# A hybrid GLA/HGRN2 diffusion layer: the work around the ends of the up-projection, and the out-projection's operand loads, in another order

## The chip, the cores and the metric

The kernel runs on one core of a Trainium2 chip. The metric is the device time of one execution in microseconds (us). The engines are TensorE (PE; its weight loads are listed apart as PEld), VectorE (DVE), ScalarE (ACT), GpSimd (POOL) and SyncE (SP, which here only issues DMAs).

## The reference

One layer of a diffusion backbone: 1024 sample tokens (a latent grid of width 64) and 128 prompt tokens, model width 1024, FFN width 2816.

```
def trunk_layer(x, mod, s_gla, s_hgrn, ...):
    shift1, scale1, gate1, shift2, scale2, gate2 = jnp.split(mod, 6, axis=-1)
    h = rmsnorm(x, norm1) * (1 + scale1) + shift1
    mix, new_gla, new_hgrn = hybrid_mixer(h, s_gla, s_hgrn, ...)
    x = x + gate1 * mix
    h = rmsnorm(x, norm2) * (1 + scale2) + shift2
    x = x + gate2 * conv_ffn(h, w_ffn_up, ffn_conv, b_ffn_conv, w_ffn_down, grid)

def hybrid_mixer(...):     # 4 GLA heads and 4 HGRN2 heads, both directions
    q_a, k_a, v_a, g_a, lr_a, q_b, f_b, i_b, g_b = jnp.split(h @ w_in, offsets, axis=-1)
    o_a, ... = bidir_scan(...);  o_h, ... = bidir_scan(...)
    merged = jnp.concatenate([o_a * silu(g_a), o_h * silu(g_b)], axis=-1)   # each normed first
    return merged @ w_out, new_gla, new_hgrn

def conv_ffn(h, w_up, conv_w, conv_b, w_down, grid):
    u = dw_conv(h @ w_up, conv_w, conv_b, grid)     # 3x3 over the grid, width 3 for the prompt
    gate, up = jnp.split(u, 2, axis=-1)
    return (jax.nn.silu(gate) * up) @ w_down
```

The layer's result goes through a last rmsnorm. mod is a product of the conditioning vector (one for the samples, one for the prompt) with w_ada.

## The kernel before

**Precision.** Every large product is made from three fp32r matmuls: both operands are split into a high part, rounded to fp32r, and the rest, and high·high, high·low and low·high are added in PSUM. A *split* is thus one ScalarE copy (L132 or L1736 for weights) and one subtraction, `split_lo` (L69), on VectorE or POOL. Names ending in h and l are the two parts.

**Stages, in the order of time:**
1. Modulation, first norm, first projections (to some 135 us).
2. The scan: six groups of heads in `ORDER` over three token blocks. Between its small matmuls (L944 lv, L1005 and L1012 for the states) the generator `stream` feeds large ones as filling: projections (L612, L626), and in the last group the out-projection (`fill_steps`, L692, matmuls L755). Weights come by a list `seq` in whose order SP loads them (`load_w`, L115), each split as soon as it is issued. `issue_after` binds an instruction behind another one; the rest of the order is left to a scheduler and to the pools.
3. The second norm and the first operands of the up stage (some 700 to 772 us).
4. The up stage: 22 columns of 128 hidden units (c = 0 to 21). A column's product is done by seven half-size products in the Strassen-Winograd manner, `up(c, p)` with p = 1 to 7, 12 matmuls each (L1751), over combined weights (slots "11", "12", "21", "22" and the sums s1 to s4) and combined token blocks (t1 to t4). `up_prompt` (L1979) does the prompt in two halves, and `prompt_columns` transposes its result. F and S are the two PSUM tiles of a column (gate and up halves); to finish them VectorE adds copies p1, u2 and p5, which ScalarE makes (L1943), L2070 and L2071 for F and L2090 for S (in column 0 `first_sums`, L1825). Product 4 of a column runs in the next column's time. Then the convolution (`conv_rows`, L1899: one ScalarE product and eight VectorE steps L1915 for each tile, `conv_prompt` L1925), silu, and POOL's product of the two halves (L2011), which goes to scratch in DRAM (scr_g). POOL also forms the sums of two columns' tokens (L1868 to L1871, scr_s) and splits the next column's weights. For column 0 the sequence on each engine is fixed by `run(engine, fn)`, which chains each instruction behind the engine's last.
5. The down stage: again seven products, of 11 pairs of columns with 12 matmuls each (`product`, L2197, matmuls L2208), whose operands are loaded in pairs and split; then the prompt (L2259), gates, the last norm.

**The places the change touches.** In group 5 of the scan (n == 5), the last w_in column (3616 + 3P) is loaded and split like the others. `fill_steps` waits for three reloaded w_out tiles `ws`, then for pairs of merged scan outputs `ms` (tag mh) and four more w_out tiles, and builds the gate of the first residual by two matmuls of a one-hot row with the modulation (L737), copied by ScalarE (L738). It then goes through six token tiles, halves, and seven f of three matmuls. For the down stage, `load_gates` (L2127) brings the modulation rows to SBUF and `make_gates` (L2131) builds four half gates by matmuls (L2139) and copies (L2140), in the middle of the first product (beside its pair 10).

The core of the loop around the scan's filling and of a split:

```
for part in range(2):
    with tc.issue_after(last.ins):
        if part == 0:
            states.step("keys")
...
nc.scalar.activation(hi, raw, AF.Copy)
split_lo(eng, lo, raw, hi)
```

## Time and profile before

| | us |
|---|---|
| median of three runs | 1539.32 (1538.26 to 1544.63) |
| the profiled execution | 1542.7 |
| its span | 1540.9 |
| PE busy in it | 1483.3 |
| DVE, ACT, POOL busy | 1147.4, 783.7, 710.4 |
| steady up stage, 860 to 1257 | PE 397.00 of 397.00 |

How to read the rows that follow in the prediction: a row of the timeline gives the start and the duration in us, the engine, the line, the operation, its output and input, the shape, and how many instructions were put together; in brackets stands how long the engine had been idle before it and which instruction, or DMA, ended that idle time. A row of the waits gives the total, how often, and the longest. A row of the windows gives for a stretch its length, the busy time of PE, PEld, DVE, ACT and POOL with the number of instructions, then the TensorE clock that was granted (1.00 is full), the mean busy share of the 16 DMA engines, and GB/s. SPq is SP issuing a DMA.

### The profile page before, as it was taken

What the parts mean: (1) busy time and instruction counts of PE and PEld (TensorE: products, weight loads), DVE (VectorE), ACT (ScalarE), POOL (GpSimd) and SP (SyncE); (2) the same over time, 40 slices, a digit from 0 to 9 for tenths busy, and PEclk for the clock granted to TensorE, in tenths of its full rate; (3) what the DMA queues carried; (4) which work ended last, traced back from release to release, by engine and by line L of the source; (5) the groups of instructions that cost most, each with busy time, mean ns of one, the idle gap of its engine ahead of it and who ended that gap; (6) DMA issues with size and microseconds to landing.
All of it is one profiled execution on the core that took longest, in us unless ns stands there. A gap on an engine that the chain in (4) does not pass through costs nothing.

```text
span 1540.9 us, 31129 instructions
## 1 busy us (share of the span) xinstructions
PE 1483.3 (96%) x12506; PEld 1258.1 (82%) x12506; DVE 1147.4 (74%) x1731; ACT 783.7 (51%) x1523; POOL 710.4 (46%) x538
## 2 busy tenths in 40 slices
PE   7999999999999999899989999999999999999997
PEld 2899989999898988677767888888888887788886
DVE  3666566665566667655689999999999999479575
ACT  3565666455454545513664444444444444467444
POOL 1512132334232240122238999999999987000001
PEclk9999999999999999999999999999999999999999
DMA  9312112336445352777641655554654665979762
GB/s 339 129 41 58 36 53 79 98 108 207 114 135 170 120 184 87 274 282 252 219 151 58 218 148 125 134 130 123 193 137 119 198 169 175 333 243 365 243 192 116
DMA packets 172939, 252.49 MB, mean 164 GB/s; under 512 B 11732, under 2 KB 113602, under 8 KB 170874
## 3 DMA queue, kind: packets, MB, share of 16 engines
q1 hardware_dynamic: 149591, 172.21, 35.0%
q0 software_dynamic: 22592, 77.60, 16.3%
q8 instruction: 98, 1.61, 0.4%
q10 hardware_dynamic: 611, 0.68, 0.1%
q14 instruction: 47, 0.39, 0.1%
HBM read 190.62 MB, written 82.90 MB: 178 GB/s over the span
## 4 chain that ended last, share of the span: by engine, by line
PE 80%; DMA 6%; DVE 5%; ACT 3%; issue 3%; POOL 2%; SPq 1%; ACTq 0%; POOLq 0%; DVEq 0%
PE u L1751 26%; PE mm L612 15%; PE xb L2208 6%; PE yb L2208 6%; PE mm L626 5%; PE x L1979 4%; PE mm L755 3%; PE lv L944 3%; PE yb L2259 2%; PE u L1521 2%; PE x L1012 2%; DVE acc L1915 2%; DMA raw<-in_w_in_dram 1%; PE mm L506 1%; DMA mh<-scr_m 1%
## 5 line engine op out<-in xcount | busy, mean ns | idle before, releaser
L1915 DVE SCALAR_TENSOR_TENSOR acc<-u,convc,acc 128x945 f32<-128x945 f32 (+2 forms) x352 | 426.8, 1218 | 7.8 <-ACT acc L1903 0.7
L69 POOL TENSOR_TENSOR wl<-raw,wh 128x1024 fp32r<-128x1024 f32 x42 | 104.1, 2480 | 237.5 <-ACT wh L132 177.4
L612 PE MATMUL mm<-h1h,wh 128*128 128x384 f32 x528 | 185.9, 352 | 0.8 <-ACT qj L515 0.8
L612 PE MATMUL mm<-h1l,wh 128*128 128x384 f32 x528 | 180.0, 341 | 0.0
L612 PE MATMUL mm<-h1h,wl 128*128 128x384 f32 x528 | 179.9, 341 | 0.0
L907 DVE TENSOR_TENSOR Q<-Q,fb 128x384 f32<-128x384 f32 x126 | 84.7, 672 | 95.0 <-PE lv L944 92.4
L69 POOL TENSOR_TENSOR wul<-sr,wuh 128x512 fp32r<-128x512 f32 (+1 forms) x64 | 116.3, 1818 | 20.1 <-ACT wuh L1736 19.9
L69 POOL TENSOR_TENSOR wul<-ra,wuh 128x1024 fp32r<-128x1024 f32 x44 | 112.4, 2554 | 20.3 <-ACT wuh L1736 17.8
L897 ACT ACTIVATE m<-k 128x384 f32<-128x384 f32 x126 | 70.2, 557 | 87.7 <-PE lv L944 41.1
L2183 POOL TENSOR_TENSOR sq<-sq,mhalf 128x1 f32<-128x1 f32 x9 | 11.1, 1231 | 214.7 <-DVE sq L2180 214.7
L612 PEld LDWEIGHTS mm<-h1h,wh 128*128 128x128 f32 x528 | 100.2, 190 | 5.7 <-issue 3.9
L612 PEld LDWEIGHTS mm<-h1l,wh 128*128 128x128 f32 x528 | 100.2, 190 | 0.6 <-issue 0.2
L612 PEld LDWEIGHTS mm<-h1h,wl 128*128 128x128 f32 x528 | 100.0, 189 | 0.8 <-issue 0.5
L626 PE MATMUL mm<-wh,h1h 128*128 128x256 f32 x288 | 83.8, 291 | 0.9 <-ACT v L651 0.9
L909 DVE TENSOR_TENSOR k<-k,fb 128x384 f32<-128x384 f32 x126 | 74.2, 589 | 12.0 <-ACT m L897 6.7
L626 PE MATMUL mm<-wh,h1l 128*128 128x256 f32 x288 | 80.5, 279 | 0.0
L626 PE MATMUL mm<-wl,h1h 128*128 128x256 f32 x288 | 80.4, 279 | 0.0
L132 ACT ACTIVATE wh<-raw 128x1024 fp32r<-128x1024 f32 x50 | 52.9, 1059 | 43.9 <-DMA raw<-in_w_in_dram 11.6
L1736 ACT ACTIVATE wuh<-ra 128x1024 fp32r<-128x1024 f32 x42 | 44.3, 1055 | 40.1 <-issue 20.5
L2011 POOL TENSOR_TENSOR acc<-acc,acc 128x1152 f32<-128x1152 f32 x22 | 60.1, 2732 | 9.7 <-DVE acc L1915 9.7
L1943 ACT ACTIVATE u2p<-u 128x512 f32<-128x512 f32 x44 | 26.4, 600 | 70.2 <-PE u L1751 70.2
L1736 ACT ACTIVATE wuh<-sr 128x512 fp32r<-128x512 f32 (+1 forms) x62 | 48.1, 775 | 24.1 <-PE x L1979 16.1
(387 smaller groups left out, 4489.4 us busy)
## 6 DMA issues: line engine op xcount, KB each, us to landing
ra<-in_w_ffn_up_dram SPq DMA_DIRECT2D x84, 256.0 KB, 3.1
raw<-in_w_in_dram SPq DMA_DIRECT2D x32, 512.0 KB, 5.2
v<-in_w_ada_dram SPq DMA_DIRECT2D x27, 512.0 KB, 4.4
scr_g<-acc POOLq DMA_DIRECT2D x22, 576.0 KB, 5.4
scr_s<-late POOLq DMA_DIRECT2D x11, 1024.0 KB, 5.8
scr_t<-in_w_ffn_down_dram POOLq DMA_DIRECT2D x16, 704.0 KB, 7.2
wa<-in_w_ada_dram SPq DMA_DIRECT2D x16, 512.0 KB, 6.3
scr_t<-in_w_ffn_down_dram POOLq DMA_DIRECT2D x2, 2816.0 KB, 13.6
```

Of the source, the lines that this page charges most:

```text
L69: return eng.tensor_tensor(out, full, hi.bitcast(F32), op=ALU.subtract)
L612: anchor["fill"] = mm(ps, a[:, kt, :], h[kt][b], start=(n == 0), stop=(n == 23))
L626: anchor["fill"] = mm(ps, h[kt][t // 3][:, ts_], a[:, kt % 4, :], start=(n == 0), stop=(n == 23))
L897: nc.scalar.activation(aps(t, 0, [[2 * h, NB], [h, 2], [1, h]]), aps(src, 0, [[2 * h, NB], [BL + h, 2], [1, h]]), AF.Copy)
L907: nc.vector.tensor_tensor(qm, qm, aps(ff_, 2 * h - 1, [[BL - h, 2], [2 * h, NB], [0, h]]), op=ALU.mult)
L909: nc.vector.tensor_tensor(km, km, aps(ff_, BL + 2 * h - 1, [[-(BL + h), 2], [2 * h, NB], [0, h]]), op=ALU.mult)
L1736: first = nc.scalar.activation(hi, raw, AF.Copy)
L1751: last = mm(dst, w_slot(c, a, x)[:, kt, :], HB[y][b][:, kt, :], start=(start and n == 0), stop=(stop and n == 11), skip_group_check=True,)
L1915: last = nc.vector.scalar_tensor_tensor(o, u3[:, r0 + dy : r1 + dy, c0 + dx : c1 + dx], wc(3 * (dy + 1) + dx + 1), o, op0=ALU.mult, op1=AL ...
L1979: last = mm(pk, HB[h]["p"][:, 4 * half + kt, :], aps(flat(W[x]), a * 512 + kt * P, [[(b - a) * 512, 2], [1, P]]), start=(half + kt + n == ...
L2011: last = nc.gpsimd.tensor_tensor(accg, accg, accu, op=ALU.mult)
L2208: anchor["down"] = mm(banks[i], w[a][:, ts_], w[b][:, 512:1024], start=(start and j == 0 and n == 0), stop=(j == NPAIR - 1 and n == 2), sk ...
```

## The change

It keeps what is computed and alters when it is done, in five places:

- **A.** The split of the last w_in column is held back (`held_cols`) and issued in group 5 behind a step of the state keys.
- **B.** `fill_steps` loads the first two operand tiles (f = 0 and 1 of token block 0) into query buffers (`me`) ahead of everything else, orders the other loads anew, replaces the gate matmuls by two broadcast DMAs from scratch, and goes through the first token tile with f outermost (`FIRST`). The second block's four loads stand together.
- **C.** Column 0 and 1 of the up stage: the weight sums s2 and s4 are formed earlier, the sums into S and F ahead of the low parts of t4, and the convolution of column 0's F is issued behind the first pair of splits. In column 1 column 2's splits stand behind the ScalarE copies, with those of "21" and "22" last.
- **D.** In the last column (c = 21) the products run in the order 5, (4 of column 20), 2, 1, 3, 6, prompt, 7, prompt, 4, transposes; it was 5, 2, 3, 1, prompt, 6, prompt, 7, transposes, 4.
- **E.** Down stage: the gates come by four broadcast DMAs (`load_gates`), the matmuls and copies are gone; the first product takes its first three pairs together (`head=3`), a bank at a time, each matmul chained behind the other.

```diff
@@ load_w
+        def split():
+            nc.scalar.activation(hi, raw, AF.Copy)
+            split_lo(eng, lo, raw, hi)
+        if slots["hold"]:
+            slots["held"].append(split)
+        else:
+            split()
...
-    seq_cols(3616 + 3 * P)
+    def held_cols():
+        slots["hold"] = True
+        w = w_cols(w_in, 3616 + 3 * P, nc.gpsimd)
+        slots["hold"] = False
+        return w
+    seq.append((1, held_cols))
@@ fill_steps
+        for f in range(2):
+            early.append(qp.tile([P, 2, BL], F32R, name="me", tag="Q"))
+            nc.sync.dma_start(early[f].bitcast(F32), scr_merged[0][0][:, f])
-        ws = list(next_ws(3))
-        ms = [load_merged(0, 0)]
+        ms = [None]
+        ws = list(next_ws(3))
+        ms.append(load_merged(0, 1))
...
-            pt = ps_mm.tile([P, 512], F32, name="mm", tag="mm")
-            mm(pt, ident[:, rr : rr + 1].to_broadcast([P, P]), modr["B"], start=True, stop=True)
-            nc.scalar.activation(gate1[1][:, j * 512 : (j + 1) * 512], pt, AF.Copy)
+            nc.sync.dma_start(gate[:, j * 512 : (j + 1) * 512], scr_mod["B"][rr : rr + 1, :].to_broadcast([P, 512]))
-                ms = [load_merged(b, p) for p in range(3)]
-            ms.append(load_merged(b, 3))
+                ms = [load_merged(b, p) for p in range(4)]
+                for half, f in FIRST if t == 0 else [(half, f) for half in range(2) for f in range(7)]:
@@ the scan
+                            if n == 5:
+                                while slots["held"]:
+                                    slots["held"].pop(0)()
@@ prompt_work, first_sums
+        run("dve", lambda: second_sum("s2", "s1", "11", ALU.subtract, nc.vector))
+        run("dve", lambda: second_sum("s4", "12", "s2", ALU.subtract, nc.vector))
...
+        run("dve", lambda: tt(S[:, 512:NS], S[:, 0:512], copies["p5"], op=ALU.add))
@@ the loop over columns
+            with tc.issue_after(anchor["copy"].ins) if c == 1 else nullcontext():
+                split_slots(n, ("s1",), nc.gpsimd)
+                split_slots(n, ("11", "12"), nc.gpsimd)
...
+            with tc.issue_after(ran["act"].ins):
+                anchor["conv"] = conv_rows(F, c, acc[c][0])
+            ran["act"] = anchor["rows"]
@@ down stage
-                    mm(pt, ident[:, rr : rr + 1].to_broadcast([P, P]), modr["C"], start=True, stop=True)
-                nc.scalar.activation(gate2[v][:, HF[half]], pt, AF.Copy)
+                    nc.sync.dma_start(gate2[v][:, HF[half]], scr_mod["C"][rr : rr + 1, :].to_broadcast([P, 512]))
...
-    product(xb, True, False, copy_bank(p1, "p1"), beside={6: load_gates, 10: make_gates})
+    product(xb, True, False, copy_bank(p1, "p1"), beside={6: load_gates}, head=3)
```

Lines of the changed kernel lie up to some 35 further down (L1008 is L1026 there, L1012 L1030, L1021 L1039, L515 L528, L897 L915, L132 L133, L1386 L1407, L1811 L1834, L1915 L1937, L2011 L2035, L1868 to L1870 L1890 to L1892).

The first place is ScalarE in group 5 of the scan (part A): kt is the key copy that TensorE's state products wait for, wh the held weight tile. Before:

```order
L132 ACTIVATE wh<-raw 128x1024 [waits DMAHW3_49,PE_49]
L515 ACTIVATE bj<-mm 128x384 [waits PE_49]
L132 ACTIVATE wh<-raw 128x1024 [waits DMAHW5_49,DMASW5_49,Pool_49]
L1008 ACTIVATE kt<-x 128x256 [waits PE_49]
L897 ACTIVATE m_8138<-k 128x384 [waits DVE_49,PE_49]
L897 ACTIVATE m_8140<-Q 128x384 [waits DVE_49,PE_49]
...
L897 ACTIVATE m_8234<-k 128x384 [waits DVE_49]
L1021 ACTIVATE st<-x 128x128 [waits PE_49]
L515 ACTIVATE qj<-mm 128x384 [waits PE_49]
L1008 ACTIVATE kt<-x 128x256 [waits PE_49]
```

And with the change:

```order
L133 ACTIVATE wh<-raw 128x1024 [waits DMAHW3_49,PE_49]
L528 ACTIVATE bj<-mm 128x384 [waits PE_49]
L1026 ACTIVATE kt<-x 128x256 [waits PE_49]
L915 ACTIVATE m_8138<-k 128x384 [waits DVE_49,PE_49]
L915 ACTIVATE m_8140<-Q 128x384 [waits DVE_49,PE_49]
...
L915 ACTIVATE m_8234<-k 128x384 [waits DVE_49]
L1039 ACTIVATE st<-x 128x128 [waits PE_49]
L133 ACTIVATE wh<-raw 128x1024 [waits DMAHW5_49,PE_49]
L528 ACTIVATE qj<-mm 128x384 [waits PE_49]
L1026 ACTIVATE kt<-x 128x256 [waits PE_49]
```

The last weight copy, which waits for its load, left the place in front of the key copy and stands behind the second transposed state (st), in front of the third key copy.

The second place is VectorE at the end of column 0 (part C): acc are token sums, sr and ra the raw weights, the adds with cp and u2p are the F and S sums. Before:

```order
L1386 TENSOR_TENSOR acc_9785<-rb_9796,acc_9785 128x1024
L1386 TENSOR_TENSOR acc_10300<-rb_9796,acc_10300 128x1024
L69 TENSOR_TENSOR wul<-sr,wuh 128x512 [waits DMAHW0_49,DVE_49,Activation_49]
L1811 TENSOR_TENSOR sr<-sr,ra 128x512 [waits DMAHW3_49]
L1811 TENSOR_TENSOR sr<-ra,sr 128x512 [waits DMAHW4_49,DVE_49]
L69 TENSOR_TENSOR t4l<-acc_9785,t4h 128x4x256
L69 TENSOR_TENSOR t4l<-acc_10300,t4h 128x4x256 [waits Activation_49]
L1842 TENSOR_TENSOR u<-u,cp_10253 128x512
L1932 SCALAR_TENSOR_TENSOR acc_9784<-x,convc,acc_9784 128x127 [waits Activation_49,Pool_49]
L1843 TENSOR_TENSOR u<-u,u2p_10304 128x512 [waits DVE_49]
L2090 TENSOR_TENSOR u<-u,u2p_10304 128x512
```

And with the change:

```order
L1834 TENSOR_TENSOR sr<-sr,ra 128x512 [waits DMAHW6_49,DVE_49]
L1834 TENSOR_TENSOR sr<-ra,sr 128x512 [waits DMAHW7_49,DVE_49]
L1407 TENSOR_TENSOR acc_9783<-rb_9794,acc_9783 128x1024
L1407 TENSOR_TENSOR acc_10298<-rb_9794,acc_10298 128x1024
L1854 TENSOR_TENSOR u<-u,u2p_10302 128x512 [waits PE_49]
L69 TENSOR_TENSOR wul<-sr,wuh 128x512 [waits DMAHW3_49,Activation_49]
L1861 TENSOR_TENSOR u<-u,cp_10251 128x512
L1862 TENSOR_TENSOR u<-u,u2p_10302 128x512 [waits DVE_49]
L69 TENSOR_TENSOR t4l<-acc_9783,t4h 128x4x256
L69 TENSOR_TENSOR t4l<-acc_10298,t4h 128x4x256 [waits Activation_49]
L1937 SCALAR_TENSOR_TENSOR acc_9782<-u,convc,acc_9782 128x15x63 [waits Activation_49]
```

The two weight sums moved ahead of the token sums, and the sums into S and F ahead of the low parts of t4; the convolution (L1937) follows at once.

The third place is POOL at the end of the up stage (parts D and E): ra, sr and raw are the loaded pairs of the first down product, acc the tiles of columns 20 and 21. Before (without the DMA issues):

```order
L69 TENSOR_TENSOR wul<-ra,wuh 128x1024 [waits DMAHW6_49,DMAHW5_49,Activation_49]
L69 TENSOR_TENSOR wul<-sr,wuh 128x1024 [waits DMAHW2_49,DMAHW7_49,PE_49,Activation_49]
L69 TENSOR_TENSOR wl_14093<-raw_14098,wh_14092 128x1024 [waits DMAHW7_49,DMAHW0_49,Activation_49]
L2011 TENSOR_TENSOR acc_10300<-acc_10300,acc_9785 128x1152 [waits DVE_49]
L69 TENSOR_TENSOR wul<-sr,wuh 128x1024 [waits DMAHW3_49,DMAHW4_49,PE_49,Activation_49]
L69 TENSOR_TENSOR wl_14095<-raw_14099,wh_14094 128x1024 [waits DMAHW2_49,DMAHW1_49,Activation_49]
L1870 TENSOR_TENSOR late<-acc_10300 128x512 [waits DMASW5_49]
L2011 TENSOR_TENSOR acc_10299<-acc_10299,acc_9784 128x1152 [waits DVE_49,Activation_49]
```

And with the change:

```order
L2035 TENSOR_TENSOR acc_10298<-acc_10298,acc_9783 128x1152 [waits DVE_49,Activation_49]
L69 TENSOR_TENSOR wul<-ra,wuh 128x1024 [waits DMAHW1_49,DMAHW0_49,Activation_49]
L69 TENSOR_TENSOR wul<-sr,wuh 128x1024 [waits DMAHW5_49,DMAHW2_49,Activation_49]
L1892 TENSOR_TENSOR late<-acc_10298 128x512 [waits DMASW5_49]
L69 TENSOR_TENSOR wl_14091<-raw_14096,wh_14090 128x1024 [waits DMAHW3_49,DMAHW2_49,Activation_49]
L69 TENSOR_TENSOR wl_14093<-raw_14097,wh_14092 128x1024 [waits DMAHW5_49,DMAHW4_49,Activation_49]
L69 TENSOR_TENSOR wul<-sr,wuh 128x1024 [waits DMAHW6_49,DMAHW7_49,PE_49,Activation_49]
L2035 TENSOR_TENSOR acc_10297<-acc_10297,acc_9782 128x1152 [waits DVE_49,Activation_49]
```

Column 20's product moved ahead of the splits of the pairs behind the first, and one pair's split (sr, with its wait on PE) went from the fourth to the sixth place.

## The prediction

> **What bounds the kernel now.** I read the busy times first, then the chain that ended last, then TensorE's own waits.

> ```profile
> PE 1483.3 (96%) x12506; PEld 1258.1 (82%) x12506; DVE 1147.4 (74%) x1731; ACT 783.7 (51%) x1523; POOL 710.4 (46%) x538
> PE 80%; DMA 6%; DVE 5%; ACT 3%; issue 3%; POOL 2%; SPq 1%; ACTq 0%; POOLq 0%; DVEq 0%
> PE x L1012 <- ACT kt L1008: 9.2, 9, 3.6
> PE u L1751 <- DVE u L2090: 6.6, 2, 5.0
> ```

> TensorE is busy 96% and is 80% of the last chain. It stands idle 1540.9 − 1483.3 = 57.6 us, and the two largest waits (total, times, longest) hold 15.8 of them. The change removes almost no matmuls, so its gain must come from such gaps, from the clock behind them, and from twelve matmul records that make gates. The steady up stage has no gap:

> ```profile
> 860.00:1257.00 397.00, 397.00 (x1944) 328.41 (x1943) 385.32 (x405) 185.02 (x247) 383.06 (x254) 1.00 0.54 150
> L1915 DVE SCALAR_TENSOR_TENSOR acc<-u,convc,acc 128x945 f32<-128x945 f32 (+2 forms) x352 | 426.8, 1218 | 7.8 <-ACT acc L1903 0.7
> ```

> In this window (first row: PE, PEld, DVE, ACT, POOL, then the clock) PE is always busy, so columns 2 to 20 neither gain nor, while their order stays, lose. Its 1944 matmuls are 17.7 columns of 110 (84 for the halves, 24 for the prompt, 2 transposes), 22.4 us each; DVE has 11.7 us of slack in them, less than one convolution step (1.218 us, second row) a column, and POOL 13.9.

> A gap also costs clock. The stretches behind the larger gaps are:

> ```profile
> 570.00:575.00 5.00, 5.00 (x18) 5.00 (x18) 4.56 (x6) 1.57 (x4) 2.30 (x1) 0.50 0.40 135
> 635.00:640.00 5.00, 3.74 (x10) 2.95 (x11) 0.89 (x2) 1.21 (x2) 0.99 (x1) 0.66 1.01 410
> 650.00:655.00 5.00, 4.52 (x16) 3.65 (x17) 2.91 (x9) 2.64 (x8) 0.00 (x0) 0.66 1.11 321
> 800.00:805.00 5.00, 3.19 (x8) 2.52 (x9) 4.51 (x9) 2.04 (x3) 5.00 (x3) 0.55 0.16 48
> 805.00:810.00 5.00, 5.00 (x19) 3.99 (x18) 4.89 (x6) 2.64 (x3) 2.53 (x3) 0.77 0.54 157
> 1285.00:1290.00 5.00, 5.00 (x16) 3.94 (x16) 4.89 (x5) 0.33 (x1) 4.92 (x4) 0.66 1.11 255
> 1320.00:1325.00 5.00, 3.52 (x11) 2.79 (x12) 2.08 (x2) 5.00 (x10) 0.00 (x0) 0.77 1.03 380
> 1325.00:1330.00 5.00, 5.00 (x21) 4.06 (x20) 2.46 (x3) 2.91 (x3) 0.00 (x0) 0.89 1.05 399
> ```

> I count (1 − clock) × busy as lost: 2.5, 1.3, 1.5, 1.4 + 1.2, 1.7, and 0.8 + 0.6 us; 11.0 in all.

> **Part A, the held split (565 to 575 us).**

> ```profile
> 568.17 1.06 ACT L132 ACTIVATE wh<-raw 128x1024 fp32r<-128x1024 f32 x1 [3.25 <-DMA raw<-in_w_in_dram]
> 569.14 0.36 ACT L1008 ACTIVATE kt<-x 128x256 f32<-128x256 f32 x1
> 569.55 1.01 PE L1012 MATMUL x<-v,kt 128*128 128x128 f32 x3 [3.65 <-ACT kt L1008]
> ```

> ScalarE sits 3.25 us in front of a weight tile that has not landed, the key copy queues behind, and TensorE waits 3.65 us for that copy. Now the weight copy stands sixteen rows later, with one other key copy and an evacuation queued behind it there; its data has then landed. Of the 3.65 us about 0.5 is the copy itself, so 3.15 go, and 2.5 of clock with them: 5.6. VectorE (4.56 busy of the next 5) is late next. Bounds: −3 if it takes over at once, −6 if even the 0.5 goes. I take **−5.5**, the rows' own sum.

> **Part B, out-projection (628 to 658, and 680).**

> ```profile
> 628.38 0.34 SPq L147 DMA_DIRECT2D wh<-scr_wo  x1
> 628.36 1.02 PE L737 MATMUL mm<-modr,ident 128*128 128x512 f32 x2
> 630.41 1.12 PE L737 MATMUL mm<-modr,ident 128*128 128x512 f32 x2
> 636.26 0.47 PE L755 MATMUL mm<-wh,mh 128*128 128x512 f32 x1 [1.85 <-DMA mh<-scr_m]
> 679.82 0.47 PE L755 MATMUL mm<-wh,mh 128*128 128x512 f32 x1 [1.58 <-DMA mh<-scr_m]
> ```

> The gate matmuls keep PE busy for 1.02 + 1.12 = 2.1 us. They become two broadcast DMAs of 256 KB. The wait at 636.26 is 1.85, and the clock 2.8. From 635 to 640 the DMA engines are full at 410 GB/s: SP lets everything go only when a weight slot frees at 628.38. Now two early tiles of 384 KB (0.8 MB, 1.9 us at that rate) go ahead of it into buffers that need no such slot, and 12 of the first tile's 42 products need only them and weights that are there; they are 12 × 0.23 = 2.7 us of cover for the rest. Of 2.1 + 1.85 + 2.8 = 6.75 I take **−6**, since 2.7 us of cover outlasts 1.85. Bounds: −3 if the queue, which carries the same bytes and the gates' 0.5 MB (1.2 us) more, paces the first tile's end anyway, and −9 if both early tiles' 1.9 us and the short key waits come on top. The second block's loads now stand together, the first ahead of the x tiles, which clears at most 1.58: **−1** (0 to −1.6).

> **Part C, column 0's end (789 to 824).**

> ```profile
> 793.25 0.69 DVE L69 TENSOR_TENSOR wul<-sr,wuh 128x512 fp32r<-128x512 f32 x1 [1.65 <-ACT wuh L1835]
> 795.19 4.51 DVE L69 TENSOR_TENSOR t4l<-acc,t4h 128x1024 fp32r<-128x1024 f32 x2
> 792.24 0.28 PE L1979 MATMUL x<-wuh,pl 128*128 128x256 f32 x1
> 801.81 0.80 PE L1751 MATMUL u<-t4h,wuh 128*128 128x512 f32 x1 [5.02 <-DVE u L2090]
> 819.48 0.50 PE L1751 MATMUL u<-t2h,wuh 128*128 128x512 f32 x1 [1.04 <-ACT cp L1943]
> 823.97 0.50 PE L1751 MATMUL u<-t3h,wuh 128*128 128x512 f32 x1 [1.47 <-ACT u2p L1943]
> L1943 ACT ACTIVATE u2p<-u 128x512 f32<-128x512 f32 x44 | 26.4, 600 | 70.2 <-PE u L1751 70.2
> ```

> TensorE waits 5.02 us, from 796.8 on, for the sum into S, last on VectorE's list. The two weight sums (1.3 of the 1.94 us between the starts of wul and t4l) move into the 1.65 us of idle, and the S and F sums go ahead of t4l. The S sum now waits for the t3 product, which PE has left by 792.24 for the prompt; the sums of F and t4l are queued behind it. But t4l (4.51, two halves beside a busy POOL) ends last, at about 799.8, and the second matmul of the t4 product needs it. The gap shrinks to 3.0 us: 2.0 won, and 0.3 by the first matmul ahead of it. A gap of 3.0 is well above the 1.85 of part B, so I leave all the slow clock in place. In column 1 the two copies go ahead of column 2's splits, and a copy itself takes 0.60, so 0.4 of the 1.04 and 0.8 of the 1.47 go. First column's convolution now stands on ScalarE ahead of two pairs of splits for column 1 (about 1 us), which PE needs only after the t4 product; I cost it at nothing, and at 1 us if that cover is gone. **−3.5**; bounds −1.5 (only the column-1 copies and a little) and −6 (clock comes back too).

> **Parts D and E, the end of the up stage and the first down products (1275 to 1330).**

> ```profile
> 1279.19 0.50 PE L1751 MATMUL u<-t4h,wuh 128*128 128x512 f32 x1 [1.57 <-DVE u L2090]
> 1273.92 1.22 DVE L1915 SCALAR_TENSOR_TENSOR acc<-u,convc,acc 128x960 f32<-128x960 f32 x1
> 1284.82 0.47 PE L2208 MATMUL xb<-wuh 128*128 128x512 f32 x1 [1.91 <-DVE acc L1932]
> 1285.28 2.78 POOL L69 TENSOR_TENSOR wl<-raw,wh 128x1024 fp32r<-128x1024 f32 x1
> 1309.91 0.32 SPq L2129 DMA_DIRECT2D modrC<-scr_modC  x1
> 1313.03 3.60 PE L2139 MATMUL yb<-modrC,ident 128*128 128x512 f32 x8
> 1316.07 0.80 PE L2208 MATMUL xb<-wuh 128*128 128x512 f32 x1
> 1316.70 0.39 PE L2208 MATMUL xb<-wul,wuh 128*128 128x512 f32 x1
> 1316.93 0.39 PE L2208 MATMUL xb<-wuh,wul 128*128 128x512 f32 x1
> 1317.23 1.06 ACT L132 ACTIVATE wuh<-sr 128x1024 fp32r<-128x1024 f32 x1 [11.09 <-DMA sr<-in_w_ffn_down_dram]
> 1321.48 0.50 PE L2208 MATMUL yb<-wh 128*128 128x512 f32 x1 [2.10 <-ACT gate L2140]
> ```

> Gone are the gate matmuls (1313.03 to 1316.07, 3.04), the wait on their copies (2.10) with 1.4 of clock, and, since the transposes now stand behind the last t4 product and other work ahead of it, the 1.91 with 1.7 of clock: 10.15. Of the 1.57 for the S sum, VectorE's turn, I give half, 0.8. On SP the load of the gate rows waited until 1309.91 with the second product's loads behind it, so ScalarE waited 11.09 for one. That wait on POOL moves to the final norm's load, ten pair loads later; behind it are pairs that PE needs over 10 us after, which hides it.

> New: the head takes pairs 0 to 2 together, so its 36 × 0.23 = 8.3 us of matmuls, from about 1282.6 to 1290.9, need all three at once, while POOL now runs column 20's gate product (2.7) ahead of the splits of pairs 1 and 2 and splits pair 3 last. VectorE ends column 20's convolution at 1275.1; POOL's list from there is that product, the splits of pairs 1 and 2, a token sum (some 1.7), and the splits of pairs 4, 5 and 3, with two DMA issues between. By an estimate of 2.6 a split (one took 2.78) pair 2 is ready near 1283.5, some 0.5 late at most, and pair 3 near 1293.4, 2.5 behind the head's end; that last gap would bring one slow stretch, 1.7. Net 10.95 − 4.7: **−6**. Bounds: −11 if POOL is in time, −1 if it is two splits (5.6) later.

> **Sum:** −5.5 − 6 − 1 − 3.5 − 6 = −22. The profiled execution took 1542.7 (span 1540.9 and 1.8 around it), 3.4 above the median of 1539.3: the sum gives 1520.7 from the one and 1517.3 from the other. I count from the middle, 1541, and forecast **1519**.

> [...] The rows show the clock at 0.66 behind gaps of 1.85 and 1.91 us, and 0.77 behind 2.10. [...]

> **Rivals.**
> 1. *The slow clock stays though the gaps go*, since what is left of them suffices (1.85 did). Then A loses 2.5, B 2.8 and E 1.4 of their gain: −15, or 1526. For it: gaps of that length are left in C and E. Against: behind 1.58 and 1.57 (679.82, 1279.19) the first matmul takes 0.50 at most, against 0.80 behind 5.02.
> 2. *New limits take over*: A −5, B −3 (DMA paces the first tile), C −2, E −2 (POOL paces the head): −12, or 1529. For it: DMA full in 635 to 640, POOL 4.92 of 5 in 1285 to 1290. Against: the early tiles leave before the full stretch.
> 3. *All pays*, POOL in time and the clock whole: −31, or 1510. For it: A's copy has nothing else to wait for. Against: t4l in C.
> 4. *It does not do what it says*: each wait is replaced by an equal one behind it (VectorE for ScalarE in A, t4l in C, POOL in E), and only the gate matmuls' 2.1 + 3.0 go: 1536. Against: in A and E the data is there long before.
> 5. *Slower*: the steady stage leaves VectorE 11.7 / 17.7 = 0.66 us of slack a column. If the new start let column 1's convolutions end so late that each S sum of the following 20 columns came one convolution step (1.2) later, the stage would lose 24 and the rest win 12: 1553. It decides once column 1's lag passes what a column can make good, 0.66 us. Against: the order of columns 2 to 20 is the old one, and the first convolution moves forward.

> **How the numbers follow.** Forecast 0.52 (1514 to 1523), rival 1 0.16, rival 2 0.12, rival 3 0.07, rival 4 0.09, rival 5 0.04. The range of 1509 to 1531 takes in the forecast, rivals 1 to 3 and the bounds of the parts but for all low or all high ends at once. A measurement of this kernel tells 0.5% (7.7 us) from no change: forecast and rivals 1 to 3 are faster (0.87), rival 4 is the same (0.09), rival 5 slower (0.04).

> **What would show it.** A: TensorE's longest wait on a key copy under 1 us, and the clock above 0.9 in the 5 us that follow. B: no gate matmuls near 628, the wait at 636 gone, the first out-projection tile done some 6 us sooner beyond A. C: the S sum gone from TensorE's waits, and one of about 3 us on t4l. E: the gate copies gone as a releaser, POOL's splits named in the head, and the second down product's first matmul (1321.48 now) some 20 us sooner. It is wrong if the steady columns take more than 22.4 us each, or if the first tile ends no sooner than A alone makes it.

## The result, and the profile after

The changed kernel took 1523.19 us (median of four runs, 1520.53 to 1526.40); the kernel before took 1538.79 beside it (four runs, 1537.11 to 1544.63). The ratio is 0.9893 with a 95% interval of 0.9859 to 0.9927: 11 to 22 us faster, where 1519 (20 us) had been forecast. A second series (below) gave 1522.44 against 1536.12, ratio 0.9906 (0.9888 to 0.9923). The profiled execution of the changed kernel took 1526.4 us, with a span of 1524.6.

The page of the changed kernel, busy times and the chain that ended last:

```profile
PE 1470.2 (96%) x12494; PEld 1250.5 (82%) x12494; DVE 1146.5 (75%) x1731; ACT 779.9 (51%) x1517; POOL 707.7 (46%) x538
PE 81%; DVE 5%; DMA 5%; ACT 3%; issue 3%; POOL 2%; SPq 0%; POOLq 0%; ACTq 0%; DVEq 0%
```

TensorE's waits in it (total, times, longest), those that answer to the rows of before:

```profile
PE x L1030 <- ACT kt L1026: 5.7, 7, 2.0
PE mm L775 <- DMA mh<-scr_m: 4.0, 3, 3.0
PE u L1772 <- DVE acc L1937: 3.4, 2, 2.6
PE u L1772 <- DVE t4l L69: 2.7, 1, 2.7
PE u L1772 <- ACT wuh L1859: 1.0, 1, 1.0
PE xb L2244 <- POOL wul L69: 0.9, 1, 0.9
```

The 3.6 us wait on a key copy, the 5.0 on the S sum, the 2.1 on the gate copies and the 1.9 on the prompt's convolution are gone. In their place stand a longer wait for the out-projection's operands (3.0 where 1.85 was), one for t4l (2.7, forecast 3.0), and one for POOL's split (0.9; 0.5 and 2.5 were forecast); two the forecast did not have, a convolution (2.6) and a weight copy (1.0). The longest wait on a key copy that is left, 2.0, stands at 390.5 us, ahead of all that was changed. From the first landmark of the table below (562 us before, 566 after) to the end, TensorE idles 29.9 us where it idled 38.0, and is busy 928.6 where it was 940.9: the larger part of what was won is shorter busy time, which is less slow clock (from 555 to 1500 us 27.3 us at 0.50 before, 13.7 after), and the gate matmuls (2.1 and 3.0).

To see where the time went I compared the times at which TensorE starts the same matmul in two profiles: those that start in the profile of before at 562.06 and 584.23 us (projections, L612), 777.50, 809.76 and 1259.82 (up stage, L1751), 1295.13 and 1330.97 (down stage, L2208). The table gives the difference from the profile of before by stretch, in us:

| profile | to 562 | 562-584 (A) | 584-777 (B) | 777-810 (C) | 810-1260 | 1260-1295 (D, head) | 1295-1331 (gates) |
|---|---|---|---|---|---|---|---|
| changed kernel | +3.97 | −6.32 | −3.96 | −1.92 | −0.56 | −0.17 | −7.49 |
| changed, again | −0.95 | −6.31 | −3.80 | −3.51 | −0.72 | −0.31 | −7.50 |
| A alone | +3.03 | −6.31 | +0.96 | +0.22 | −0.64 | +0.05 | −1.71 |
| gates alone | +1.11 | −0.97 | −0.73 | +0.23 | −0.59 | +0.04 | −7.51 |
| head alone | +0.34 | −2.22 | +0.45 | −0.21 | −0.59 | −3.78 | +5.02 |
| old last column | −2.49 | −6.31 | −4.40 | −1.69 | −0.65 | −3.76 | −7.09 |
| product 3 first | +0.02 | −6.32 | −4.42 | −2.08 | −0.74 | −2.99 | −7.48 |
| no early tiles | −0.10 | −6.32 | +0.19 | −3.54 | −0.67 | +1.12 | −7.50 |
| early tiles once | +0.80 | −6.30 | +0.60 | −1.96 | −0.10 | −0.33 | −7.49 |
| POOL late | −0.18 | −6.31 | −3.87 | −5.74 | −0.65 | −0.09 | −7.50 |
| s1 first | +0.48 | −6.32 | −3.51 | −3.02 | −0.58 | −0.10 | −7.49 |
| combination | +2.14 | −6.31 | −4.00 | −6.86 | −0.81 | −3.77 | −7.12 |

Up to 562 us each engine of all these kernels runs the same instructions in the same order, so the second column is chance: −2.5 to +4.0 us between executions. A few us of difference between two medians can thus be chance. Each stretch repeats to a few tenths where the same amount of slow clock falls into it, which is what the experiments are read by.

### The profile page after: what moved, and what is told of

The parts are those of the page before. It is cut to its first block, busy times and chain, and to the rows that moved or that the text cites. A ratio compares the mean times of both kernels' runs of the same rounds, so it can differ in the third digit from the quotient of the medians.

```text
span 1524.6 us, 31105 instructions
## 1 busy us (share of the span) xinstructions
PE 1470.2 (96%) x12494; PEld 1250.5 (82%) x12494; DVE 1146.5 (75%) x1731; ACT 779.9 (51%) x1517; POOL 707.7 (46%) x538
## 4 chain that ended last, share of the span: by engine, by line
PE 81%; DVE 5%; DMA 5%; ACT 3%; issue 3%; POOL 2%; SPq 0%; POOLq 0%; ACTq 0%; DVEq 0%
PE u L1772 26%; PE mm L625 15%; PE xb L2244 7%; PE yb L2244 6%; PE mm L639 5%; PE x L2003 4%; PE mm L775 3%; PE lv L962 3%; PE yb L2296 2%; PE u L1542 2%; PE mm L519 1%; PE x L1030 1%; DVE acc L1937 1%; DMA mh<-scr_m 1%; DMA wa<-in_w_ada_dram 1%
## 5 line engine op out<-in xcount | busy, mean ns | idle before, releaser
L1937 DVE SCALAR_TENSOR_TENSOR acc<-u,convc,acc 128x945 f32<-128x945 f32 (+2 forms) x352 | 426.8, 1218 | 7.3 <-ACT acc L1925 0.2
L69 POOL TENSOR_TENSOR wl<-raw,wh 128x1024 fp32r<-128x1024 f32 x42 | 102.4, 2444 | 249.8 <-ACT wh L133 195.5
L69 POOL TENSOR_TENSOR wul<-sr,wuh 128x512 fp32r<-128x512 f32 (+1 forms) x64 | 119.6, 1868 | 16.5 <-ACT wuh L1757 16.4
L69 POOL TENSOR_TENSOR wul<-ra,wuh 128x1024 fp32r<-128x1024 f32 x44 | 115.2, 2617 | 19.1 <-ACT wuh L1757 19.1
L915 ACT ACTIVATE m<-k 128x384 f32<-128x384 f32 x126 | 70.2, 557 | 81.9 <-PE lv L962 39.4
L133 ACT ACTIVATE wh<-raw 128x1024 fp32r<-128x1024 f32 x50 | 52.8, 1058 | 42.2 <-PE mm L625 11.4
L2035 POOL TENSOR_TENSOR acc<-acc,acc 128x1152 f32<-128x1152 f32 x22 | 61.1, 2779 | 15.1 <-DVE acc L1937 15.1
L639 PEld LDWEIGHTS mm<-wh,h1h 128*128 128x128 f32 x288 | 55.1, 191 | 3.4 <-issue 1.7
```

What stands on the lines that cost most here:

```text
L69: return eng.tensor_tensor(out, full, hi.bitcast(F32), op=ALU.subtract)
L639: anchor["fill"] = mm(ps, h[kt][t // 3][:, ts_], a[:, kt % 4, :], start=(n == 0), stop=(n == 23))
L915: nc.scalar.activation(aps(t, 0, [[2 * h, NB], [h, 2], [1, h]]), aps(src, 0, [[2 * h, NB], [BL + h, 2], [1, h]]), AF.Copy)
L1937: last = nc.vector.scalar_tensor_tensor(o, u3[:, r0 + dy : r1 + dy, c0 + dx : c1 + dx], wc(3 * (dy + 1) + dx + 1), o, op0=ALU.mult, op1=AL ...
L2035: last = nc.gpsimd.tensor_tensor(accg, accg, accu, op=ALU.mult)
```

## The experiments

Each kernel was timed beside the kernel before on the same chip.

| run | median us | before us | ratio, 95% interval |
|---|---|---|---|
| A alone | 1536.31 | 1539.41 | 0.9979 (0.9968 to 0.9991) |
| gates alone | 1532.70 | 1539.41 | 0.9956 (0.9938 to 0.9975) |
| old last column | 1519.64 | 1539.41 | 0.9865 (0.9846 to 0.9885) |
| product 3 first | 1520.35 | 1539.41 | 0.9871 (0.9855 to 0.9888) |
| head alone | 1541.03 | 1541.33 | 1.0004 (0.9989 to 1.0020) |
| no early tiles | 1530.23 | 1541.33 | 0.9923 (0.9902 to 0.9944) |
| POOL late | 1519.00 | 1541.33 | 0.9858 (0.9839 to 0.9877) |
| s1 first | 1522.88 | 1541.33 | 0.9881 (0.9865 to 0.9897) |
| changed, again | 1522.44 | 1536.12 | 0.9906 (0.9888 to 0.9923) |
| combination | 1515.40 | 1536.12 | 0.9855 (0.9839 to 0.9871) |
| early tiles once | 1528.08 | 1536.12 | 0.9940 (0.9924 to 0.9956) |

**A alone.** The kernel before with `held_cols` and the call in group 5:

```diff
-    seq_cols(3616 + 3 * P)
+    seq.append((1, held_cols))
...
                             states.step("keys")
+                            if n == 5:
+                                while slots["held"]:
+                                    slots["held"].pop(0)()
```

> The kernel before with part A alone: the last w_in split held back into group 5. Theory (the parts add up, and A is worth what its stage shows, 3.97 + 2.34 = 6.3 us between 562 and 584): 6 us faster than the kernel before, TensorE's longest wait on a key copy under 1.1 us. Rival (the scan paces itself on VectorE, so the gain is given back before the up stage): under 3 us.

Measured: 6.31 less in the stage, against the profile of before; in the median 3.1 (1.4 to 4.9). In place of the 3.65 us wait and the slow clock behind it, TensorE is busy throughout at full clock:

```profile
566.00:571.00 5.00, 5.00 (x82) 4.34 (x81) 3.08 (x7) 2.52 (x5) 2.38 (x1) 1.00 1.05 383
571.00:576.00 5.00, 5.00 (x80) 4.40 (x79) 3.17 (x7) 1.65 (x4) 0.00 (x0) 1.00 0.85 265
```

Up to the up stage 0.96 us is lost again. That A gives it back, as the rival has it, is not shown: the clock is at 0.50 for 10.2 us of that stretch, where it was for 6.8 in the profile of before, and this alone costs 1.7. Why the 6.31 is larger than the median's gain lies in part in the profile of before. In the two other profiles in which this place is unchanged, TensorE's wait on the key copy and ScalarE's on the weight read (first row and third: gates alone; second: head alone, PE):

```profile
570.72 0.71 PE L1012 MATMUL x<-v,kt 128*128 128x128 f32 x4 [3.70 <-ACT kt L1008]
568.70 0.71 PE L1012 MATMUL x<-v,kt 128*128 128x128 f32 x4 [2.45 <-ACT kt L1008]
569.34 1.06 ACT L132 ACTIVATE wh<-raw 128x1024 fp32r<-128x1024 f32 x1 [3.25 <-DMA raw<-in_w_in_dram]
```

They were 1.0 and 2.2 us faster through the same stage, once with less slow clock (0.66 in the 5 us behind the wait, where it was 0.50 before) and once with a load that came sooner. So A is worth 4 to 6 us where it stands. The mechanism of the theory holds; its 6 us, outside the median's interval, was that of one slow execution.

**Gates alone.** The kernel before with the changed `load_gates` in place of `make_gates`:

```diff
-    product(xb, True, False, copy_bank(p1, "p1"), beside={6: load_gates, 10: make_gates})
+    product(xb, True, False, copy_bank(p1, "p1"), beside={6: load_gates})
```

> The kernel before with the four broadcast DMAs for the second gates in place of the matmuls and copies, but without the first product's head of three pairs and with the old order of the last column. Theory: the matmuls (3.04), the wait on the copies (2.10) and the clock behind it (1.4) go, 6.5 us or the 7.5 of the stage. Rival (the loads of the second product set its start, and the head and the last column's order helped them): 3 us or less, with a wait on DMA or ScalarE in place of the copies' one.

Measured: −7.51 in the stretch from 1295, the same as in the changed kernel, and 6.7 in the median. The theory holds, and the rival falls. Of the 7.5, 1.7 is slow clock behind the copies' wait in the profile of before (0.66 in the 5 us behind it); in the profile of A alone the same wait (2.02) was followed by full clock, and against that one the gates give 5.8. In the changed kernel the second product begins without a wait:

```profile
1306.81 0.39 PE L2244 MATMUL yb<-wh 128*128 128x512 f32 x1
```

**Old last column.** Part D undone in the changed kernel:

```diff
-        if c == NHID:
-            up(c - 1, 4)
-            prompt_columns(c - 1)
-            second_half(c - 1)
-        elif c > 0:
+        if c > 0:
...
-        last_c = c == NHID - 1
+        last_c = False
```

> The changed kernel with the old order of products in the last column (part D undone), head and gates kept. Theory (D gains its 5 us and gives as much back: 2.64 us for p1, the clock behind it, 0.89 for POOL's split): within 1.5 us of the changed kernel, about 15 us faster than before; the 1.57 and 1.91 us waits come back and the 2.64 goes. Rival (D is what opens the way for the down stage): 5 us slower than the changed kernel.

Measured: 3.6 us faster than the changed kernel in the stretch from 1260 (−3.76 against −0.17), and in the median 19.8 faster than before, where the changed kernel was 15.6 in its own series. Both expectations fail: D is not neutral, it costs. TensorE's waits of over 0.6 us from 1240 us to the second down product, in the changed kernel (first two rows) and with the old last column (third):

```profile
1257.01 0.80 PE L1772 MATMUL u<-b11h,wuh 128*128 128x512 f32 x1 [2.64 <-DVE acc L1937]
1285.14 0.50 PE L2244 MATMUL xb<-wul,wuh 128*128 128x512 f32 x1 [0.89 <-POOL wul L69]
1263.67 0.50 PE L1772 MATMUL u<-t4h,wuh 128*128 128x512 f32 x1 [1.57 <-DVE u L2131]
```

The wait of 1.91 us on the prompt's convolution is absent from both. I had put its absence down to D's order of transposes; it is gone without D.

**Product 3 first.** Only p3 and p1 of the last column exchanged again:

```diff
             up(c, 2)
-            if not last_c:
-                up(c, 3)
+            up(c, 3)
...
             up(c, 1)
-            if last_c:
-                up(c, 3)
```

> The changed kernel with product 3 again ahead of product 1 in the last column, the rest of D kept. Theory: p1 waits because its bank is still read by column 20's convolution on VectorE; 2.7 us of product 3 ahead of it cover the 2.64 us wait and most of the slow clock behind it, so 3 to 4.5 us faster than the changed kernel, some 19 us faster than before. Rival (VectorE, busy without a break there, is the bound, and the wait only moves to the sum into S or to the transposes): within 1 us of the changed kernel.

Measured: 2.8 us faster than the changed kernel in the stretch (−2.99 against −0.17). The 2.64 us wait is gone; POOL's split is 1.34 late in place of 0.89. This is a little under the theory's 3 to 4.5, and 2.8 of the 3.6 that D costs: product 1, moved ahead of 3, met a bank that column 20's convolution still read.

**Head alone.** The kernel before with `head=3` and the chained matmuls, old gates:

```diff
-    product(xb, True, False, copy_bank(p1, "p1"), beside={6: load_gates, 10: make_gates})
+    anchor["down"] = ran["pe"]
+    product(xb, True, False, copy_bank(p1, "p1"), beside={6: load_gates, 10: make_gates}, head=3)
```

> The kernel before with only the first down product's head of three pairs, old gates and old last column. Theory (after the run with the old last column, where the 1.91 us wait was gone without D: a bank's turn comes three pairs later, so its matmuls no longer meet the prompt's convolution that still reads the memory of that bank): the 1.91 and the 1.7 of clock behind it go, 3.6 us between the first and the 41st matmul of the stage, about 3.5 us faster than before. Rival (D or the broadcast gates made room): under 1 us, the wait still there.

Measured: the 1.91 us wait is gone and the stretch is 3.78 faster, as the theory has it, and yet the kernel is not (1.0004). In the timeline the old gates now wait, and SP's load of the gate rows goes when POOL's last token sum ends:

```profile
1305.49 2.15 POOL L1871 TENSOR_TENSOR late<-acc,late 128x512 f32<-128x512 f32 x1
1307.67 0.33 SPq L2129 DMA_DIRECT2D modrC<-scr_modC  x1
1310.64 5.37 PE L2139 MATMUL yb<-modrC,ident 128*128 128x512 f32 x8 [3.04 <-DMA modrC<-scr_modC]
```

In the profile of before that sum ended at 1309.88 and the load went at 1309.91: with the head both are 2.2 earlier, as all ahead of the stage is, and the head has not moved them. With the old gates the end of the first product was thus held by that load, and TensorE was just not waiting for it. What the head wins it loses there again, with slow clock behind the new wait (0.66 in 5 us; +5.02 in the last stretch). The head needs the new gates, and they do not need it: gates alone give 7.5, head alone loses 1.2, both (old last column) give 10.9 in the two stretches.

**No early tiles.** Out-projection without the query-buffer tiles:

```diff
-            early.append(qp.tile([P, 2, BL], F32R, name="me", tag="Q"))
-            nc.sync.dma_start(early[f].bitcast(F32), scr_merged[0][0][:, f])
...
-        ms = [None]
         ws = list(next_ws(3))
+        ms = [load_merged(0, 0)]
```

> The changed kernel without the two early operand tiles in query buffers; the first merged pair is loaded as the second, ahead of the third weight tile was before it and behind the weight reload, gates still by DMA, f outermost in the first token tile. Theory (the full DMA queue sets the end of the first tile, so the early tiles are worth only their 0.8 MB, 1.9 us at 410 GB/s): 2 us slower than the changed kernel, all of it before the 45th product of the out-projection. Rival (the cover of 12 products carries part B): 4 us or more slower.

Measured: 4.2 us slower than the changed kernel at the up stage (+0.19 against −3.96). VectorE's evacuations (`ev<-mm,gate`) show where: without the early tiles the first token tile is done 1.6 us later than in the changed kernel (chance up to 562 us taken off), block 0 1.0 later, and the first half tile of block 1 5.1 later. The theory sized the first tile (2) about right and missed the rest; the rival has the sum and the wrong place. SP's loads of block 1 (mh), in the changed kernel (first three rows) and without early tiles:

```profile
641.36 1.78 SPq L729 DMA_DIRECT2D mh<-scr_m  x1
644.20 21.46 SPq L765 DMA_DIRECT2D v<-in_x_sample_dram  x3
670.95 1.69 SPq L729 DMA_DIRECT2D mh<-scr_m  x2
641.70 20.34 SPq L761 DMA_DIRECT2D v<-in_x_sample_dram  x3
666.50 3.04 SPq L725 DMA_DIRECT2D mh<-scr_m  x3
```

In the changed kernel one of the three goes at 641, since the early tiles leave one of three merged buffers free, and two at 671. Without them all three go at 666.5, behind the x tiles, and TensorE waits for them:

```profile
672.80 0.47 PE L771 MATMUL mm<-wh,mh 128*128 128x512 f32 x1 [2.84 <-DVE up L1320]
```

(The row names a VectorE sum that ended at that moment; the semaphore that this matmul waits for is that of the load issued at 666.50.) In the last column this kernel loses 1.3 more than the changed one (+1.12 against −0.17), in two waits on POOL's splits of 1.89 and 1.79; why POOL is later there was not followed up.

**Early tiles once.** A run to tell the buffer from the cover: the first token tile reads the early tiles, and the first pair is also loaded into its usual buffer for tiles 1 and 2:

```diff
             if f == 6:
                 ms.append(load_merged(0, 3))
+                ms[0] = load_merged(0, 0)
...
-                        lhs = early[f][:, a, ts_] if b == 0 and f < 2 else ms[f // 2][:, f % 2, a, ts_]
+                        lhs = early[f][:, a, ts_] if t == 0 and f < 2 else ms[f // 2][:, f % 2, a, ts_]
```

> The changed kernel, but with the first merged pair also loaded into its usual buffer (0.79 MB more, behind the loads of the first token tile) and used there by token tiles 1 and 2; only the first token tile reads the early tiles. Theory (the early tiles pay because they leave a third merged buffer free, so that block 1's first load starts before block 0 is done): now that load waits for TensorE again, 3 to 5 us slower than the changed kernel, lost between the 128th product of the out-projection and the up stage, and the first tile ends as early as in the changed kernel within 1 us. Rival (the cover of the first 12 products is what pays): within 1.5 us of the changed kernel at the start of the up stage.

Measured: 4.6 us slower than the changed kernel at the up stage (+0.60 against −3.96), 5.6 in the median. The first tile is done 2.5 us later (expected: 1 at most), since the extra 0.79 MB stand ahead of the last weight tile; block 0 ends 1.8 later, and the first half tile of block 1 4.4 later. That jump of 2.6 stands at this wait, with block 1's loads issued at 668.25:

```profile
668.25 3.04 SPq L729 DMA_DIRECT2D mh<-scr_m  x3
675.14 0.47 PE L776 MATMUL mm<-wh,mh 128*128 128x512 f32 x1 [3.43 <-DMA mh<-scr_m]
```

Two kernels without the free buffer lose 4.1 and 2.6 us just where block 1 begins, one of them with the early tiles still in use. (The first has the clock at 0.66 in the 5 us behind its wait, the second at 1.00, which is 1.7 us of work.) So the theory holds for the place and the sum, the buffer is worth that much, and the cover of the first tile is worth at most the 1.6 us.

**POOL late.** One small POOL sum that reads t4l, and the splits chained behind it:

```diff
+        run("pool", lambda: nc.gpsimd.tensor_tensor(one_c, HB["l"]["t4"][:, 3, 511:512].bitcast(F32), one_c, op=ALU.add))
...
-            ran["act"], ran["pool"] = split_slots(1, names, nc.gpsimd, both=True)
+            ran["act"], ran["pool"] = split_slots(1, names, nc.gpsimd, both=True, behind=ran["pool"])
```

> The changed kernel with POOL's three weight splits of column 1 held until t4l is done, by one small POOL sum that reads t4l (its result, written over a constant of 1.0 whose last use is past, is not used again). Theory (POOL's splits beside it double t4l, 2.26 us an instruction against 1.2): t4l takes 2.4 in place of 4.5, the 2.75 us wait falls below 1, the clock behind it holds, and the wait of column 1 for POOL's splits does not appear: 3 to 4 us faster than the changed kernel between the 83rd product of the up stage and the next prompt. Rival (POOL's splits, 2.2 us later, are late for column 1): no gain, a wait on POOL of about 1 to 2 us in its place.

The two halves of t4l on VectorE, and POOL's first two splits, in the changed kernel (first three rows) and in this one (last three):

```profile
790.21 4.52 DVE L69 TENSOR_TENSOR t4l<-acc,t4h 128x1024 fp32r<-128x1024 f32 x2
790.48 3.17 POOL L69 TENSOR_TENSOR wul<-ra,wuh 128x1024 fp32r<-128x1024 f32 x1 [19.11 <-ACT wuh L1757]
793.62 3.37 POOL L69 TENSOR_TENSOR wul<-sr,wuh 128x1024 fp32r<-128x1024 f32 x1
786.17 2.35 DVE L69 TENSOR_TENSOR t4l<-acc,t4h 128x1024 fp32r<-128x1024 f32 x2
788.93 2.41 POOL L69 TENSOR_TENSOR wul<-ra,wuh 128x1024 fp32r<-128x1024 f32 x1
791.30 2.40 POOL L69 TENSOR_TENSOR wul<-sr,wuh 128x1024 fp32r<-128x1024 f32 x1
```

Measured: −5.74 in the stretch against −1.92, so 3.8 us, and no wait on POOL. The wait on t4l is down to 0.56. Of the 3.8, 1.6 is the clock: against the two profiles in which it held in this stretch without this edit (−3.51 and −3.54) the gain is 2.2. Side by side, both subtracting tiles, VectorE took 4.52 for the two halves (1.22 and 3.39) and POOL 3.17 and 3.37 for its splits; one after the other they took 2.35, and 2.41 and 2.40.

**s1 first.** The copy of s1's high part moved ahead of the first high part of t4:

```diff
-        half_hi("t4", 0, tmp[2])
         slot = SLOT[1]["s1"]
...
         run("act", lambda: nc.scalar.activation(hi, raw, AF.Copy))
+        half_hi("t4", 0, tmp[2])
```

> The changed kernel with the high part of column 1's s1 copied on ScalarE ahead of the two high parts of t4. Theory (moving the two weight sums ahead pushed the t4 sums back by 1.3 us, and s1's copy stood behind one of them, so TensorE waited 1.00 us for it): that wait goes and t4l ends 1 us sooner: 1 us faster in the stage, hardly to be told in the median. Rival (TensorE then waits 1 us longer for t4l): no change.

Measured: −3.02 in the stretch against −1.92, 1.1 us, with slow clock behind the t4l wait in both (0.66 in the 5 us behind it); the wait on s1's copy is gone while that on t4l stays at 2.76. The theory holds.

**The changed kernel again.**

> The changed kernel once more, in five rounds, as the reference for the runs beside it. Theory (its first profile began 4.0 us late in code that the change does not touch, and the profile of before was itself 3 us slow behind that): 17 to 20 us faster than before, and the same ledger of stages from 562 us on, −20.5 against the profile of before within 2 us. Rival (the 4.0 us are part of the change): they appear again, and the median is 15 to 16 us faster.

Measured: −0.95 up to 562 us, so the 4.0 us of the first profile were chance, and the stretches behind it sum to −22.2 (−20.4 in the first profile). The median is 13.7 faster, less than expected: the theory is right about the ledger (the sum of the stretches). The median lies nearer to the rival's 15 to 16, but the 4.0 us on which the rival rests did not come again.

**The combination.** Old last column, POOL late and s1 first together.

> The changed kernel with the old last column, POOL's column-1 splits behind t4l, and s1's copy ahead of those of t4. Theory (the three act in different places and add up: 3.6 + 3.7 + 0.6): 8 us faster than the changed kernel, 25 to 27 us faster than before, with t4l and s1 gone from TensorE's larger waits. Rival (t4l begins sooner with s1 first, but POOL's splits then set column 1): the sum falls 2 to 3 us short.

Measured: 1515.40 us, 7.0 faster than the changed kernel on the same chip and 20.7 faster than before. In the ledger C gives −6.86 and the end −3.77, which is what the three gave alone (3.8 + 1.1 + 3.6), and neither t4l nor s1 is among TensorE's larger waits. The theory that the three add up holds, within 1 us of its 8; its 25 to 27 against before does not, since the changed kernel's own median gain was 13.7 and not 17 to 20.

## Why the prediction was right, and where it was not

The direction, the bound (gaps of TensorE) and the range (1509 to 1531) were right; 1523.2 lies just past the slow end of the forecast's own 1514 to 1523. Of the forecast −22 the profiles show −20.4 and −22.2, the medians −15.6 and −13.7. That the profiles come so near to the sum is in part luck, since its terms were off both ways.

- **The base and the clock.** The step that failed is "I count (1 − clock) × busy as lost" as a gain that is sure. From 555 us on, over all 13 profiles, a gap on TensorE of 1.8 to 3.7 us was followed by 5 us of slow clock in 31 cases of 40. The profile of before (1542.7 us, 3.9 and 6.6 above the medians of its kernel in the two series) had it behind every one of its gaps from 1.85 up. The same gap of the same kernel, the 2.64 us wait for b11h, in the changed kernel (first two rows) and in its second profile, in intervals of 3.41 us (PE's busy time stands behind the length; the clock is the third number from the end):

```profile
1253.48:1256.89 3.41, 0.89 (x4) 0.38 (x3) 3.20 (x6) 0.53 (x2) 3.41 (x3) 1.00 1.02 191
1256.89:1260.30 3.41, 3.29 (x8) 2.62 (x9) 3.34 (x4) 1.17 (x1) 2.29 (x3) 0.50 0.87 342
1245.89:1249.30 3.41, 1.97 (x9) 1.31 (x7) 3.16 (x6) 1.61 (x3) 3.41 (x4) 1.00 0.98 165
1249.30:1252.71 3.41, 2.21 (x10) 1.83 (x11) 3.38 (x4) 1.17 (x1) 2.79 (x3) 1.00 0.97 342
```

  In the clock records of the traces every slow stretch between 555 and 1500 us is 3.41 us at 0.50, or two or three such pieces in a row. Those of the changed kernel's first profile start at 632.25 (6.83 long), 796.09 and 1256.89 (3.41 each), and from the first of them to the others it is 48 and 183 times 3.413 us. Counted in such intervals, the gap falls into one in the first profile here (2.53 idle, then 0.50), and into two in the second (1.44 and 1.20, then 1.00). So, as I read it, what looks like chance is where the gap falls (the last section has the counts).

  A piece holds back 3.41 × 0.5 = 1.7 us of work, but that is lost only if nothing behind it waits for another engine. Here it cost 0.1 (−0.17 against −0.31 in the stretch): with the clock whole, TensorE waited 0.90 us for the sum into S, for which it did not wait in the first profile, and 1.10 in place of 0.89 for POOL's split. Behind the t4l wait, with the clock at 0.66 in one profile and 1.00 in the other, it cost 1.6 (−1.92 against −3.51). With 6.7 us of clock in the sum, this and the slow profile of before are a good part of the 6 to 8 us between sum and medians. That they are all of it is only argued: the 4 us of chance ahead of 562 us are as large.
- **A**, forecast −5.5: right in place, −6.3 against this profile, 4 to 5 against the two others. It passed its own bound of −6: the 0.5 kept back for the copy went too, and so did 2.7 us of busy time for the 2.5 counted. VectorE did not take over.
- **B**, −6 and −1: it gave 4.0 and 3.8 against the profile of before, in place of 7, and 4.9 and 4.8 against A alone, in which this stretch has 1.7 more of slow clock. None of the 2.8 us of clock came, as rival 1 has it for B: the clock is at 0.50 for 6.8 us of this stretch before and in both profiles of the changed kernel. By the evacuations the two win, against A alone, 4.7 and 4.3 in the first tile, give 0.7 back in the rest of block 0, and win 0.8 and 1.1 where block 1 begins, about as forecast there. The step that failed is "2.7 us of cover outlasts 1.85": the wait was not covered but grew, because the twelve early products began at 624, while the loads behind the weight slot were released only then and took until 633.6:

```profile
624.17 0.34 SPq L153 DMA_DIRECT2D wh<-scr_wo  x1
633.63 0.76 PE L775 MATMUL mm<-wh,mh 128*128 128x512 f32 x1 [3.03 <-DMA mh<-scr_m]
633.63:638.63 5.00, 5.00 (x58) 3.80 (x59) 1.23 (x4) 0.32 (x2) 0.00 (x0) 0.50 1.01 421
```

  The DMA engines, full in the 5 us ahead of that product too (1.03 busy, 405 GB/s), set the first tile, as rival 2 had it. From the freeing of the weight slot to the first product on these loads it is 9.5 us, against 7.9 before (628.38 to 636.26), though the same two weight halves stand ahead of the load; why it takes longer is not shown. Without the early tiles the first tile kept 3.1 us of its gain, so the gates and the order by f carry most of that; which of the two was not tried. And the −1 was right for a reason I had not seen: block 1's first load goes early only because the early tiles leave a buffer free, and without that block 1 loses.
- **C**, −3.5: −1.9, or −3.5 where the clock held. The last agrees by luck: the forecast left all slow clock in place, and TensorE's idle time in the stretch fell by 1.3 alone (5.72 to 4.47 and 4.37); the rest is clock, at 0.50 for 6.8 us before, for 3.4 and for none in the two profiles. The t4l wait came as worked out (2.75 for 3.0), behind one matmul:

```profile
788.29 0.50 PE L1772 MATMUL u<-t1h,wuh 128*128 128x512 f32 x1 [1.00 <-ACT wuh L1859]
794.79 0.50 PE L1772 MATMUL u<-t4l,wuh 128*128 128x512 f32 x1 [2.75 <-DVE t4l L69]
```

  Not seen: the weight sums, put into the idle 1.65 us, pushed the t4 sums and the s1 copy behind them back, which cost 1.00 (the first row; without it in the run with s1 first). The two copies of column 1 won 0.3 and 0.8 as forecast, but column 2's first product now waits 0.77 for a convolution. The step "move into the 1.65 us of idle" failed: that idle time was a wait for the s1 copy, and what fills it from ahead pushes the copy back.
- **D and E**, −6: −7.7, right in size with two wrong parts in it. The 1.91 went by the head, not by D; D costs 3.6, and 2.8 of it by a wait on a bank that I did not look for when product 1 moved ahead of 3. The gates gave 7.5 for 6.5, of which 1.7 is the clock of the profile of before. POOL's pair 3 was ready at 1285.1, 8.3 us before the 1293.4 worked out, where all ahead of the last column ran 8.8 earlier; TensorE waited 0.9 for it and not 2.5; as I read it, its own wait for the bank and the clock behind that had made it late too.
- **Rival 5** (VectorE in the steady stage) did not occur: the steady columns changed by −0.6 us, in kernels with and without part C alike.

## What to carry to other kernels

Read a gap's worth from the work behind it: of a wait that is taken away, look up in the order what else the same waiter needs, and price the bank, buffer or slot that the moved instruction takes as well as the one it leaves. Count slow clock behind a gap as a chance (31 of 40 here), not as a sum, and count it only where no other engine sets what follows; take more than one profile before one is made the base. Of two edits at one place one may be worth nothing by itself and 3.4 us beside the other (10.9 against 7.5), so test them apart and together.
